# RMSNorm with SiLU on one core: stores moved to GpSimd's software queue, gamma's row in a tile of its own, three squares moved to VectorE

## The chip, the cores and the metric

One core of a Trainium2 chip. The metric is device time in microseconds (us) of one execution, lower is better. The span of a profile is the part between the first and the last instruction; it is 1.7 to 2.1 us shorter than the time of the same execution.

## The reference

```python
def setup_inputs():
    batch, seq_len, hidden = 8, 1024, 2048
    ...                      # x, gamma: normal float32; eps = 1e-5

def reference(x, gamma, eps):
    rms = np.sqrt(np.mean(x ** 2, axis=-1, keepdims=True) + eps)
    out = gamma * x / rms
    return (out * (1 / (1 + np.exp(-out)))).astype(np.float32)
```

So 67.1 MB are read, 67.1 MB are written, and each element needs a square, a scaling and a Silu.

## The kernel before

The 8192 rows are cut into 16 blocks of 512 rows (J = 4 rows on each of 128 partitions, 4.194 MB). A block is loaded by SyncE's queue into one of six buffers, worked on in place, and stored from the same buffer. A load of block b + 6 therefore waits for the store of block b.

```python
def sums(b, after_first=()):
    ss = small.tile([P, J], f32, name="ss")
    na = J // 2
    for j in range(na, J):                       # two rows on VectorE
        nc.vector.tensor_tensor_reduce(out=junk_v, in0=row(b, j), in1=row(b, j), ...,
                                       accum_out=ss[:, j:j + 1])
    for j in range(na):                          # two rows on ScalarE
        nc.scalar.activation(out=junk_a, in_=row(b, j), func=ACT.Square, accum_out=ss[:, j:j + 1])
        if j == 0:
            for s in after_first:
                store(s)                         # stands behind this square in ScalarE's queue
    ...                                          # rms = sqrt(ss / d + eps)

def finish(b, halves=False):
    for j in range(J):
        nc.vector.scalar_tensor_tensor(out=row(b, j), in0=row(b, j), scalar=rstds[b][:, j:j + 1],
                                       in1=g, op0=ALU.mult, op1=ALU.mult)
        if j % 2:
            cols = slice((j - 1) * d, (j + 1) * d)
            nc.scalar.activation(out=blocks[b][:, cols], in_=blocks[b][:, cols], func=ACT.Silu)
            if halves:
                nc.scalar.dma_start(out=ob[b][:, cols], in_=blocks[b][:, cols])

def store(b):
    nc.scalar.dma_start(out=ob[b], in_=blocks[b])
    if b + LEAD < nblk:                          # LEAD = 6
        load(b + LEAD)

...                                              # loads, gamma spread by a matmul, blocks 0 and 1
for b in range(1, last - 1):
    sums(b + 1, after_first=[b - 1])
    finish(b)
    invert(b + 1)                                # rstd = 1 / rms on VectorE
store(last - 2); finish(last - 1); store(last - 1)
sums(last); invert(last); finish(last, halves=True)
```

Before the change the row of gamma uses a sixth buffer of the block pool first, so the sixth load waits for it.

## Time and profile before

| | before |
|---|---|
| time, median of 3 runs | 317.48 us (317.22 to 317.64) |
| span of the profiled run (another execution, 318.03 us) | 316.3 us |
| VectorE (DVE) / ScalarE (ACT) busy | 223.5 / 223.8 us, 71% each |
| bytes moved by DMA | 134.25 MB, mean 425 GB/s |
| store to store in the middle | 19.35 us |

How to read it: an engine that is busy 71% can be idle because it waits for data or because it waits for another engine. The row of the DMA engines decides between these. It gives the mean busy share of 16 DMA engines per slice; a 9 says 90% or more, and the windows view gives the exact share. The lines are in the prediction.

### The profile page before, as it was taken

The numbers are of one execution on the slowest core, as the hardware profiler recorded it, in microseconds if no ns is written. First come the engines' busy times: TensorE is split into PE (matmuls) and PEld (weight loads), VectorE is DVE, ScalarE is ACT, GpSimd is POOL, SyncE is SP. The second block draws the span as 40 slices with busy tenths as digits, with TensorE's granted clock in tenths as the row PEclk, the third lists the DMA queues.
The fourth block names the chain that finished last, engine by engine and source line by source line (L and its number), as shares of the span: only waits on it lengthen the run. The fifth ranks groups of instructions, "written<-read, shape, count | busy, mean of one in ns | idle before, by whom it ended". The sixth has DMA issues, their size and how long they took to land.

```text
span 316.3 us, 444 instructions
## 1 busy us (share of the span) xinstructions
PE 2.1 (1%) x8; PEld 0.5 (0%) x8; DVE 223.5 (71%) x147; ACT 223.8 (71%) x144; POOL 0.2 (0%) x4
## 2 busy tenths in 40 slices
PE   0200000000000000000000000000000000000000
PEld 0000000000000000000000000000000000000000
DVE  0679499999493983939849397593966939993900
ACT  1357958999967777678676687676786776879540
POOL 0000000000000000000000000000000000000000
DMA  8999999999999999999999999999999999999996
GB/s 328 402 464 410 452 390 410 452 419 443 439 424 452 411 452 410 452 414 456 406 456 414 448 414 448 439 423 452 414 452 410 452 414 456 406 456 410 452 407 269
DMA packets 4763, 134.25 MB, mean 425 GB/s; under 512 B 532, under 2 KB 532, under 8 KB 536
## 3 DMA queue, kind: packets, MB, share of 16 engines
q1 hardware_dynamic: 2304, 67.11, 49.7%
q10 hardware_dynamic: 2456, 67.12, 49.2%
q14 instruction: 3, 0.02, 0.0%
HBM read 67.12 MB, written 67.11 MB: 424 GB/s over the span
## 4 chain that ended last, share of the span: by engine, by line
DMA 74%; DVE 14%; ACT 5%; issue 2%; DVEq 1%; ACTq 0%; SPq 0%
DMA xt<-in_x_dram 44%; DMA out_dram<-xt 30%; DVE xt L84 11%; ACT xt L88 3%; DVE junk_v L64 3%; ACT junk_a L68 1%; DVEq L164 1%; ACT L74 0%; ACT rms L74 0%; DVE rstd L79 0%; ACTq L93 0%; DVE ss L64 0%; SPq L52 0%; DVEq L64 0%; ACTq L74 0%
## 5 line engine op out<-in xcount | busy, mean ns | idle before, releaser
L84 DVE SCALAR_TENSOR_TENSOR xt<-xt,rstd,g 128x2048 f32<-128x2048 f32 x64 | 146.2, 2347 | 0.1
L88 ACT ACTIVATE xt<-xt 128x4096 f32<-128x4096 f32 x32 | 115.4, 3615 | 36.8 <-DVE xt L84 36.7
L64 DVE CUSTOM_DVE_ANT_0 junk_v<-xt 128x2048 f32<-128x2048 f32 x32 | 73.5, 2298 | 56.1 <-DMA xt<-in_x_dram 55.5
L68 ACT ACTIVATE junk_a<-xt 128x2048 f32<-128x2048 f32 x32 | 60.1, 1879 | 29.2 <-DMA xt<-in_x_dram 28.3
L74 ACT ACT_TABLE_LOAD x15 | 19.2, 1283 | 9.9 <-DVE ss L64 9.9
L88 ACT ACT_TABLE_LOAD x15 | 19.2, 1283 | 3.1 <-DVE xt L84 2.9
L79 DVE RECIPROCAL rstd<-rms 128x4 f32<-128x4 f32 x16 | 2.8, 172 | 11.3 <-ACT rms L74 11.3
L114 DVE COPY g<-junk_v 128x2048 f32<-128x2048 f32 x1 | 2.3, 2292 | 9.2 <-PE junk_v L112 9.2
L68 ACT ACTIVATION_READ_ACCUMULATOR junk_a<-xt 128x1 f32 x32 | 6.0, 186 | 0.0
L74 ACT ACTIVATE rms<-ss,eps_t 128x4 f32<-128x4 f32 x16 | 4.8, 297 | 1.2 <-DVE ss L64 1.1
L64 DVE DVE_READ_ACCUMULATOR2_ANT ss<- 128x1 f32 x32 | 4.5, 141 | 0.0
L112 PE MATMUL junk_v<-xt,ones 1*128 1x512 f32 x8 | 2.1, 1133 | 8.1 <-DMA xt<-in_gamma_dram 8.1
L107 ACT ACT_TABLE_LOAD x1 | 1.3, 1283 | 0.7 <-PEq L150 0.7
L105 DVE MEMSET ones<- 128x128 f32 x1 | 0.2, 165 | 0.8 <-PEq L150 0.8
L112 PEld LDWEIGHTS junk_v<-xt,ones 1*128 1x128 f32 x8 | 0.5, 306 | 8.1 <-issue 8.1
L107 ACT ACTIVATE junk_a<-ones 128x1 f32<-128x1 f32 x1 | 0.2, 174 | 0.0
L150 POOL MEMSET const-uint8-127<- 128x1 uint8 x1 | 0.1, 102 | 0.0
L150 POOL MEMSET const-bfloat16-1.0<- 128x1 bf16 x1 | 0.1, 101 | 0.0
L150 POOL MEMSET const-float32-0.0<- 128x1 f32 x1 | 0.1, 98 | 0.2 <-issue 0.2
L150 POOL MEMSET const-float32-1.0<- 128x1 f32 x1 | 0.1, 98 | 0.0
L106 DVE MEMSET eps_t<- 128x1 f32 x1 | 0.1, 59 | 0.0
## 6 DMA issues: line engine op xcount, KB each, us to landing
xt<-in_x_dram SPq DMA_DIRECT2D x16, 4096.0 KB, 42.0
out_dram<-xt ACTq DMA_DIRECT2D x15, 4096.0 KB, 35.2
out_dram<-xt ACTq DMA_DIRECT2D x2, 2048.0 KB, 10.4
xt<-in_gamma_dram ACTq DMA_DIRECT2D x1, 8.0 KB
```

The lines of the kernel that those rows point to most:

```text
L64: nc.vector.tensor_tensor_reduce(out=junk_v, in0=row(b, j), in1=row(b, j), scale=1.0, scalar=0.0, op0=ALU.mult, op1=ALU.add, accum_out=ss[ ...
L68: nc.scalar.activation(out=junk_a, in_=row(b, j), func=ACT.Square, accum_out=ss[:, j:j + 1])
L74: nc.scalar.activation(out=rms, in_=ss, func=ACT.Sqrt, scale=1.0 / d, bias=eps_t)
L79: nc.vector.reciprocal(out=rstd, in_=rmss.pop(b))
L84: nc.vector.scalar_tensor_tensor(out=row(b, j), in0=row(b, j), scalar=rstds[b][:, j:j + 1], in1=g, op0=ALU.mult, op1=ALU.mult)
L88: nc.scalar.activation(out=blocks[b][:, cols], in_=blocks[b][:, cols], func=ACT.Silu)
L105: nc.vector.memset(ones, 1.0)
L107: nc.scalar.activation(out=junk_a[:, 0:1], in_=ones[:, 0:1], func=ACT.Square)
L112: nc.tensor.matmul(junk_v[:, c * w:(c + 1) * w], ones[k:k + 1, :], grow[k:k + 1, 0:w], start=True, stop=True)
L114: nc.vector.tensor_copy(out=g, in_=junk_v)
L150: nc = _bacc.Bacc("TRN2", target_bir_lowering=False, num_devices=1)
L164: with _tile.TileContext(nc) as tc:
```

## The change

Its intent: ScalarE should no longer issue DMAs, a store should not wait behind a square whose block has not been loaded, the sixth load should not wait for gamma, and ScalarE should be relieved of three squares.

```diff
+    Q = 4
+    w = d // Q
+    grow = singles.tile([P, w], f32)
...
-        na = J // 2
+        na = 1 if b % 5 == 2 else 2
...
-                    nc.scalar.dma_start(out=ob[b][:, cols], in_=blocks[b][:, cols])
+                    nc.gpsimd.dma_start(out=ob[b][:, cols], in_=blocks[b][:, cols])

     def store(b):
-        nc.scalar.dma_start(out=ob[b], in_=blocks[b])
+        nc.gpsimd.dma_start(out=ob[b], in_=blocks[b])
...
-        grow = pool.tile([P, J * d], f32, name="xt")
-        for b in range(BUFS - 1):
+        for b in range(BUFS):
             load(b)
...
-        load(BUFS - 1)
```

(The cut lines only remove `Q` and `w` from their old place and replace `grow[..., 0:w]` by `grow[..., :]`.)

## The prediction

> **What bounds the kernel now.** I read the page first: busy shares, the 40 slices and the DMA queues; then the windows view with its DMA share; then the chain of waits; then the timeline of the start, of one steady block and of the end. From the page:
>
> ```profile
> PE 2.1 (1%) x8; PEld 0.5 (0%) x8; DVE 223.5 (71%) x147; ACT 223.8 (71%) x144; POOL 0.2 (0%) x4
> ...
> DMA  8999999999999999999999999999999999999996
> ...
> q1 hardware_dynamic: 2304, 67.11, 49.7%
> q10 hardware_dynamic: 2456, 67.12, 49.2%
> ```
>
> The reader is to see that VectorE (DVE) and ScalarE (ACT) are idle 29% of the span, while the DMA row is full in 38 of 40 slices and the two queues (q1 and q10) together take 98.9% of what 16 engines have. The windows view says the same for stretches of steady state (us, then the busy times, the clock, the DMA share and GB/s):
>
> ```profile
> 142.80:181.50 38.70, 0.00 (x0) 0.00 (x0) 27.60 (x18) 28.18 (x19) 0.00 (x0) 1.00 1.00 434
> 290.00:295.00 5.00, 0.00 (x0) 0.00 (x0) 3.23 (x3) 2.96 (x4) 0.00 (x0) 1.00 1.00 433
> 305.00:308.00 3.00, 0.00 (x0) 0.00 (x0) 0.00 (x0) 0.00 (x0) 0.00 (x0) 1.00 1.01 431
> 313.00:314.00 1.00, 0.00 (x0) 0.00 (x0) 0.00 (x0) 0.00 (x0) 0.00 (x0) 1.00 0.24 98
> ```
>
> The DMA share is 1.00 in the middle and still 1.00 with every compute engine idle, at 305 to 308 us. The last data packets are done at about 313.3 us; the last 3.0 us of the 316.3 us span are the acknowledgement and the end of the program. A block of 4.194 MB in and 4.194 MB out takes 19.35 us (successive stores are issued at 123.44, 142.80, 162.17, 181.52), that is 8.389 MB / 19.35 us = 433.5 GB/s. All 134.25 MB at that rate are **309.7 us**. Of the other 6.6 us of the span, 1.2 us are before the first packet, 3.0 us after the last, and some 2.4 us are slightly slower stretches (426 GB/s in 270 to 290 us, 419 in 40 to 60). The chain of waits goes from store to load and back through the reused buffers:
>
> ```profile
> 139.42 42.02 DMA xt<-in_x_dram
> 181.44 0.02 issue
> 181.46 0.03 ACT junk_a L68
> 181.48 0.04 issue
> 181.52 35.20 DMA out_dram<-xt
> ```
>
> A load needs 42.0 us and a store 35.2 us though either would take 4.194 MB / 433.5 GB/s = 9.7 us alone: both queue in a saturated DMA. The chain also shows why the author moved the store: it is issued only once the square of a later block may run, which waits for a load.
>
> **What the Trainium skill says.** (1) "DMA: Bandwidth & Descriptors", section "Where 436 GB/s comes from", puts the ceiling of the 16 ports at 435.2 GB/s; the 433.5 here is within 0.4% of it, so the trace agrees that there is no rate left to win. (2) The same page, "Queues, rings and completion order", says that each DMA engine takes turns between the queues that have work, a whole packet at a time. With both directions on hardware queues the trace agrees with an even split: at 36.67 us, when the first store is issued, the loads have had about 35.4 us x 0.43 MB = 15.2 MB; the six first loads are 25.2 MB, the missing 10.0 MB at half rate (0.217 MB per us) take 46 us, which gives 82.8 us, and the square of block 5 that had waited for its load starts at 84.02. How a packet of the software queue compares in size no run here shows yet. (3) The same page, "Latency and other measured facts", gives about 0.6 us to the first byte for the hardware queue and about 1 us for the software one: 0.4 us more per store; the trace has no software store. (4) "SBUF — State Buffer", section "SBUF: two separate sides", warns that VectorE in a two-port mode keeps GpSimd from writing its descriptors. The squares here take 2298 ns and the scalings 2347 ns for 2048 float32, about one element per ns, so they do not look like a doubled mode, and I expect no such stall; no run here shows it.
>
> **The change part by part.**
> - *Stores leave ScalarE's queue.* ScalarE loses 17 issues of 0.34 us = 5.8 us of its sequencer, all but one beside the DMA. In the end piece one stood on the chain of waits: the issue at 285.68 held the square of block 15 from 285.66 to 286.06, **0.4 us**. GpSimd gains 17 issues; it was idle (0.2 us busy). Each store pays about 0.4 us more to its first byte, perhaps 1 us with the hop to GpSimd (estimate from the skill's 1 us).
> - *A store no longer waits for a later load.* In steady state the second Silu of a block ends at 117.61 + 3.60 = 121.2, the store went at 123.44. Now it can start its data some 1.2 to 2.2 us earlier. It joins a queue that holds 35.2 / 19.35 = 1.8 stores already, so nothing is moved faster. At the start the Silu of block 0 ends at 32.70 and its store went at 36.67; now it is about 33.7, 3 us earlier. As the loads then share sooner, they land up to 3 us later, and later stores could come sooner by as much: the DMA does the same bytes in another order.
> - *Three squares on VectorE in blocks 2, 7 and 12.* VectorE gains 3 x (2.30 + 0.14) = 7.3 us, to 231 us; ScalarE loses 3 x (1.88 + 0.19) = 6.2 us, to 218 us. In a steady block VectorE has 13.8 of 19.36 us busy; with one square more it is 16.2, still 3.1 us under. Hidden. In block 2, in the ramp where VectorE is full (19.93 of 20 us at 40 to 60), it puts stores 1 and 2 some 2.4 us later, about what the earlier store 0 had won; both queues stay fed by the loads in hand.
> - *Gamma's row in its own tile.* The sixth load no longer waits for the row's use (4.8 us and 2.2 us in the waits of SyncE's queue). It stands behind five loads of 9.7 us each, 48 us of work, so it starts no sooner. Gain 0.
> - *End.* What counts is whether the last half store still finds the DMA busy. Before:
>
> ```profile
> 300.25 0.34 ACTq L90 DMA_DIRECT2D out_dram<-xt  x1
> 301.13 3.62 ACT L88 ACTIVATE xt<-xt 128x4096 f32<-128x4096 f32 x1 [0.91 <-DVE xt L84]
> 304.77 0.34 ACTq L90 DMA_DIRECT2D out_dram<-xt  x1
> ```
>
> It was issued at 304.77 and landed 10.2 us later at the earliest; 2.10 MB alone need 4.8 us plus about 2.3 us of start and acknowledgement, so it had some **3 us of slack** behind earlier stores. Shifts: -0.4 us (ScalarE's issue gone), +0.4 to 1 us (software queue), 0 to +2.7 us if loads land later by what store 0 gains. The sum, 0 to +3.3 us, is about the slack, so the end moves by 0 to 0.5 us.
>
> Sum: nothing from the steady state, nothing from the start, between -0.2 and +0.5 us at the end. From 317.48 I take **317.6 us**.
>
> **The rivals.**
> - *Stores get the larger share of the DMA.* If the software queue's packets hold several rows, a store drains fast and the loads wait. For: point (2) above leaves the size open. Against: in the page both hardware queues have one row of 32 KB per packet (2304 packets for 16 loads are 144 each, 128 rows and 16 small ones), and software may do the same. Then the last load lands when 16 loads and about 13.5 stores are through: 29.5 x 9.68 + 1.5 = 287 us, the one before at 267.7. From that landing VectorE needs 4.9 us (two squares), 9.1 us (block 13) and 9.3 us (block 14), to 291 us; before, it took from 282.0 to 304.77, 22.8 us, from there to the last issue, so now 313.8. Adding 1 + 4.8 + 2.3 + 1.3 us gives a span of some 323 us, a time of **324**, +2%.
> - *Loads get the larger share.* They land early, stores pile up, the DMA stays full to the end. The bound is then 309.7 + 1.2 + 3.0 plus the 1.2 us between span and time = 315.1 us; **315 to 317**.
> - *The software queue is slower as such* (descriptors written into on-chip memory, some DMA engines burdened by fetching them, or held up by VectorE). As all 16 engines carry equal bytes, one engine 2% slower sets the whole: 2% of 310 us is 6 us, **323 to 324**. For: it is the one new mechanism. Against: each descriptor moves 32 KB, so its own cost is small beside 32 KB / 27.1 GB/s = 1.2 us.
> - *A real gain.* If the late store were what starved the loads, issuing it early would cut the chain. Against: the DMA share of 1.00. Even with every gap but start and end gone the time is 315.1, -0.8%.
>
> **Range and chances.** The lower edge is just above the floor of 315.1; the upper one takes in most of a shared-out-of-balance tail. 315.4 to 322.0. Faster by over 2% means under 311.1, below the floor: 0.02. Slower by over 2% means over 323.8, what the first and third rivals reach only in full: 0.12. The rest, 0.86.
>
> **What would show it.** Right: a DMA share of 1.00 and 432 to 435 GB/s in the middle, 19.35 us from store to store, GpSimd issuing at the second Silu's end, VectorE near 231 us busy and ScalarE near 218, waits for loads merely shifted. Wrong: a lower rate in the middle (third rival); stores that land in 15 us with loads over 55 us and an idle DMA before the last store (first rival); or a rate above 435 GB/s, which would overturn the bound itself.

## The result, and the profile after

The changed kernel took **318.02 us** (median of 6 runs, 317.60 to 318.52), the kernel before 317.70 us (6 runs in all, 317.22 to 317.90). The ratio is 1.0012, with a 95% interval of 0.9999 to 1.0025: the same. Here and below a ratio is the mean time of one kernel's fast runs over that of the other's of the same rounds, so it isn't quite the ratio of the medians that are quoted.

The page of the changed kernel, the lines that answer to those of the prediction:

```profile
PE 2.1 (1%) x8; PEld 0.5 (0%) x8; DVE 230.5 (73%) x153; ACT 217.4 (69%) x138; POOL 9.4 (3%) x21
...
DMA  8999999999999999999999999999999999999996
...
q1 hardware_dynamic: 2304, 67.11, 49.7%
q0 software_dynamic: 2448, 67.11, 49.2%
```

VectorE has gained 7.0 us, ScalarE has lost 6.4 us, GpSimd (POOL) has 17 issues. The DMA row is digit for digit that of before, and the software queue q0 has taken the place of q10, with the same share. Its 2448 packets for 17 stores are 144 each, as on the hardware queues.

Windows of the changed kernel (columns as in the prediction: busy time of PE, PEld, DVE, ACT and POOL, clock, DMA share, GB/s):

```profile
159.20:197.90 38.70, 0.00 (x0) 0.00 (x0) 27.59 (x18) 28.20 (x18) 1.04 (x3) 1.00 1.00 434
305.00:308.00 3.00, 0.00 (x0) 0.00 (x0) 0.00 (x0) 0.00 (x0) 0.00 (x0) 1.00 1.01 431
313.00:314.00 1.00, 0.00 (x0) 0.00 (x0) 0.00 (x0) 0.00 (x0) 0.00 (x0) 1.00 0.43 180
```

The middle moves 434 GB/s as before, and the data end in the same microsecond, between 313 and 314. The timeline of its end:

```profile
298.65 0.53 POOL L93 DMA_DIRECT2D out_dram<-xt  x1 [13.51 <-ACT xt L91]
299.27 3.62 ACT L91 ACTIVATE xt<-xt 128x4096 f32<-128x4096 f32 x1 [0.91 <-DVE xt L87]
303.18 0.53 POOL L93 DMA_DIRECT2D out_dram<-xt  x1 [3.99 <-ACT xt L91]
```

The last half store is issued at 303.18, 1.6 us earlier than before (304.77), and lands 11.5 us later, where it had been 10.6 (this store alone, by the source view of its line; the 10.2 of the prediction is the other half store's). So it lands at 314.7 instead of 315.4. The last Silu ends 1.9 us sooner (302.89 against 304.75) and the kernel doesn't end sooner: the store waits longer in the DMA, and from its landing to the end of the span pass 1.5 us, where it had been 0.9. This last difference goes with the queue: 0.8 to 0.9 us in the profiles with stores on the hardware queue whose last landing is known (the kernel before, its quarter version and the hardware copy), 1.4 to 1.6 us in seven with stores on the software queue, and 1.9 us in the eighth (run 3).

The chain of waits, which had led through loads and stores before, puts 89% of the span of the changed kernel down to "issue", that is to nothing it can name. With the stores on GpSimd it no longer connects a store with the load that waits for it. A chain that breaks like this is no finding about the kernel. The issues of the page still show the queueing, first before (size of one, median us from issue to landing):

```profile
xt<-in_x_dram SPq DMA_DIRECT2D x16, 4096.0 KB, 42.0
out_dram<-xt ACTq DMA_DIRECT2D x15, 4096.0 KB, 35.2
```

and after:

```profile
xt<-in_x_dram SPq DMA_DIRECT2D x16, 4096.0 KB, 39.4
out_dram<-xt POOLq DMA_DIRECT2D x15, 4096.0 KB, 37.1
```

Load and store together stand in the DMA for 77.2 us before and 76.5 us after, or four blocks at 19.35 us.

### The profile page after: what moved, and what is told of

Its sections match the earlier page's. It is cut to its first block, busy times and chain, and to the rows that moved or that the text cites. A ratio compares the mean times of both kernels' runs of the same rounds, so it can differ in the third digit from the quotient of the medians.

```text
span 316.2 us, 463 instructions
## 1 busy us (share of the span) xinstructions
PE 2.1 (1%) x8; PEld 0.5 (0%) x8; DVE 230.5 (73%) x153; ACT 217.4 (69%) x138; POOL 9.4 (3%) x21
## 3 DMA queue, kind: packets, MB, share of 16 engines
q0 software_dynamic: 2448, 67.11, 49.2%
## 4 chain that ended last, share of the span: by engine, by line
issue 89%; DMA 4%; POOL 3%; POOLq 0%
DMA xt<-in_x_dram 4%; POOL out_dram L96 2%; POOLq L163 0%; POOL out_dram L93 0%; POOLq L96 0%; POOLq L93 0%
## 5 line engine op out<-in xcount | busy, mean ns | idle before, releaser
L67 DVE CUSTOM_DVE_ANT_0 junk_v<-xt 128x2048 f32<-128x2048 f32 x35 | 80.4, 2298 | 47.5 <-DMA xt<-in_x_dram 46.8
L71 ACT ACTIVATE junk_a<-xt 128x2048 f32<-128x2048 f32 x29 | 54.4, 1876 | 23.9 <-DMA xt<-in_x_dram 23.5
L96 POOL DMA_DIRECT2D out_dram<-xt x15 | 8.1, 542 | 276.6 <-ACT xt L91 276.6
L112 PE MATMUL junk_v<-grow,ones 1*128 1x512 f32 x8 | 2.1, 1131 | 8.3 <-DMA grow<-in_gamma_dram 8.3
L93 POOL DMA_DIRECT2D out_dram<-xt x2 | 1.1, 533 | 17.5 <-ACT xt L91 17.5
```

Source lines behind the costliest of these rows:

```text
L93: nc.gpsimd.dma_start(out=ob[b][:, cols], in_=blocks[b][:, cols])
L96: nc.gpsimd.dma_start(out=ob[b], in_=blocks[b])
L112: nc.tensor.matmul(junk_v[:, c * w:(c + 1) * w], ones[k:k + 1, :], grow[k:k + 1, :], start=True, stop=True)
```

## The experiments

My theory: the DMA is full, its bytes set the time, and what the change does to engines and issue times cannot be seen. The rivals: two effects cancel (the software queue costs something and the early stores or the moved squares win it back); or arithmetic and waits bind together with the DMA.

**1. The queue alone** (before, with the two `dma_start` lines on GpSimd).

```diff
-        nc.scalar.dma_start(out=ob[b], in_=blocks[b])
+        nc.gpsimd.dma_start(out=ob[b], in_=blocks[b])
```

> Only the issuing queue is changed: stores through GpSimd, squares and gamma as before. Theory (the DMA's 134.25 MB set the time, the software queue moves them as fast): 317.7 within 0.6 us, DMA share 1.00 in the middle at 433 to 434 GB/s. Rival (two effects cancel: the software queue costs something and the early stores or the moved squares win it back): clear of before by over 1 us (0.3%), in the opposite direction to the run with the rest alone.

317.74 us (5 runs, before 317.81), ratio 1.0002 (0.9990 to 1.0015). **2. The rest alone** (the changed kernel, with the same lines back on ScalarE):

> The squares and gamma's tile as in the changed kernel, stores back on ScalarE's queue where they were. Theory: 317.7 within 0.6 us. Rival (effects cancel): off by over 1 us, with the sign opposite to the queue alone.

317.51 us, ratio 0.9989 (0.9976 to 1.0003). Neither is a microsecond off, so there are no two effects of that size that cancel; effects of half a microsecond would stay within these intervals. Gamma's tile was never run apart from the squares. The queue-only trace also answers a question of the prediction. Its timeline has store 0, store 1 and the square that waited for the load of block 5:

```profile
33.07 0.67 POOL L93 DMA_DIRECT2D out_dram<-xt  x1 [32.63 <-ACT xt L88]
56.16 0.53 POOL L93 DMA_DIRECT2D out_dram<-xt  x1 [22.42 <-ACT xt L88]
...
84.17 1.88 ACT L68 ACTIVATE junk_a<-xt 128x2048 f32<-128x2048 f32 x1 [0.39 <-DMA xt<-in_x_dram]
```

In the kernel before the same square stands in the timeline as

```profile
84.02 1.88 ACT L68 ACTIVATE junk_a<-xt 128x2048 f32<-128x2048 f32 x1 [0.29 <-DMA xt<-in_x_dram]
```

Store 0 goes out 3.6 us earlier than before (36.67), yet the load lands at the same time, to 0.15 us. Store 1 cannot follow sooner (56.16, before 55.81), as its own Silu ends only then. What store 0 took from the loads early, they get back while the store queue is empty: from 56 to 60 us that queue moves 0.00 MB and the loads 1.57 MB, where before the stores had 0.59 and the loads 1.05 MB (DMA view of these windows). From 33 to 84 us the sums are alike again, 11.83 MB for loads and 9.93 for stores, before 11.76 and 9.86. In the stretch from 60 to 100 us the DMA queues of this trace had 51.4% of the engines for stores and 48.9% for loads; before, 51.0% and 49.0%. The software queue gets the same turn as the hardware one.

**3. Stores that go out late** (the changed kernel; a small copy in front of each whole-block store waits for the block three further on; the line that makes its one-column tile `gate` is cut).

```diff
+        if b + 3 < nblk:
+            nc.gpsimd.tensor_copy(out=gate, in_=blocks[b + 3][:, 0:1])
         nc.gpsimd.dma_start(out=ob[b], in_=blocks[b])
```

> The changed kernel, but each store waits until the load of the block three further on has landed (a copy of one column by GpSimd in front of it), so in the middle stores go out some 15 to 19 us later than in the changed kernel. Theory: with about three blocks still queued in the DMA it stays full, 318.0 within 1 us, DMA share 1.00 in the middle, store to store 19.35 us. Rival (the time of a store's issue matters, early stores hide a cost of the software queue): over 2 us slower than the changed kernel.

318.42 us (4 runs), ratio to before 1.0023 (1.0009 to 1.0037); the changed kernel has 1.0012. In its trace the store of block 7 is issued at 174.56 instead of 159.17, 15.4 us late. The issues of its page:

```profile
xt<-in_x_dram SPq DMA_DIRECT2D x16, 4096.0 KB, 28.9
out_dram<-xt POOLq DMA_DIRECT2D x15, 4096.0 KB, 28.3
```

Now 57.2 us or three blocks stand in the DMA instead of four, and that is still enough to keep it full (436 GB/s from 140 to 200 us). Stores issued 15 us later move the time by 0.1% against the changed kernel. Against the kernel before it is 0.2%, some 0.7 us, and this interval leaves 1 out: small, but not nothing.

**4 to 6. A quarter of the stores**: the DMA is relieved, with wrong results. Each store sends one row of four (83.9 MB in all): the kernel before, the changed kernel, and the kernel before with the queue alone changed. The last two stores, of half a block each, send half a row (their lines are cut).

```diff
-        nc.scalar.dma_start(out=ob[b], in_=blocks[b])
+        nc.scalar.dma_start(out=ob[b][:, 0:d], in_=blocks[b][:, 0:d])
```

> The kernel before, storing only a quarter of each block (wrong result on purpose): 83.9 MB instead of 134.2 MB. Theory (bytes bind the kernel, compute has room): at 433.5 GB/s the bytes need 193.5 us, so the bound passes to VectorE: 13.72 us per block as in the ramp of the kernel before, the last store issued near 249 us, time about 255 us (250 to 260). Rival (the stores' wait on a later load, or compute, binds): above 300 us.

> The changed kernel with the same quarter stores. Theory: with the DMA out of the way the three extra VectorE squares are on the path: 3 x 2.44 = 7.3 us more than the kernel before with quarter stores, about 262 us; the software queue itself within 1 us. Rival (GpSimd's early stores help once the DMA is free): as fast as or faster than the kernel before with quarter stores.

> The kernel before with the queue alone changed and quarter stores. Theory: within 1 us of the kernel before with quarter stores (the store's latency is off the path but for the last one; 0.4 us of ScalarE's issue gained, 0.4 to 1 us of first byte lost). Rival (the software queue is costly in itself, hidden only by the full DMA): over 2 us slower.

The kernel before takes 254.43 us, the changed one 261.98, the queue alone 255.33 (4 runs each; ratios to the full kernel before 0.8010, 0.8248 and 0.8040, each within 0.0014). Taking away bytes alone, with all arithmetic left, took away 63 us. Then the bound passes to the arithmetic, as this window of the quarter kernel before shows:

```profile
100.00:200.00 100.00, 0.00 (x0) 0.00 (x0) 99.76 (x66) 99.36 (x66) 0.00 (x0) 1.00 0.91 376
```

VectorE is busy 99.76 and ScalarE 99.36 of 100 us, and the DMA is no longer full (0.91). Here the changed kernel's extra squares on VectorE are on the path, though ScalarE is relieved of them. It is 7.6 us slower, of which the queue alone makes 0.9 us and the rest 6.7 us; three squares are 3 x 2.44 = 7.3 us. So in its own terms the change carries a cost that the full DMA hides.

The 0.9 us of the queue come from the end. Windows around the last store of the quarter kernel before,

```profile
249.00:250.00 1.00, 0.00 (x0) 0.00 (x0) 0.00 (x0) 0.06 (x1) 0.00 (x0) 1.00 0.09 37
250.00:251.00 1.00, 0.00 (x0) 0.00 (x0) 0.00 (x0) 0.00 (x0) 0.00 (x0) 1.00 1.01 410
```

and of the one with the queue changed:

```profile
249.00:250.00 1.00, 0.00 (x0) 0.00 (x0) 0.00 (x0) 0.18 (x1) 0.53 (x1) 1.00 0.00 0
250.00:251.00 1.00, 0.00 (x0) 0.00 (x0) 0.00 (x0) 0.00 (x0) 0.00 (x0) 1.00 0.45 184
251.00:252.00 1.00, 0.00 (x0) 0.00 (x0) 0.00 (x0) 0.00 (x0) 0.00 (x0) 1.00 0.84 340
```

The last Silu ends at 249.07 and 249.18; on the hardware queue the data move through the whole microsecond after 250, on the software queue they begin within it. GpSimd starts to issue 0.3 us after the Silu and takes 0.53 us instead of 0.34; the store lands 2.9 us after its issue instead of 2.6, and the span ends 1.5 us after that instead of 0.9. With the 0.1 us of the later Silu these make up the 1.3 us between the two spans (252.6 and 253.9 us; the profiled execution with the queue changed was the slowest of its four). So the largest part, 0.6 us, comes after the landing.

**7 and 8. The last store sent later**, to measure its slack (the changed kernel, with idle squares on ScalarE in front of the very last Silu).

```diff
+                if halves and j == 3:
+                    for _ in range(2):               # 5 in the second run
+                        nc.scalar.activation(out=junk_a, in_=blocks[b][:, 2 * d:3 * d], func=ACT.Square)
                 nc.scalar.activation(out=blocks[b][:, cols], in_=blocks[b][:, cols], func=ACT.Silu)
```

> The changed kernel with two idle squares (1.88 us each) on ScalarE before the very last Silu, 0.9 us of which fall into a gap: the last half store goes out some 2.9 us later. Theory (it waits behind earlier stores, slack some 3.9 us: data end 313.4, less 4.84 us of its own data, less about 1.5 us to its first byte, less the issue at 303.2): no change, within 0.6 us of the changed kernel. Rival (the compute chain of the end sets the time): +2.9 us.

> The same with five squares: the last half store some 8.5 us later. Theory: slack of 3.9 us used up, the time rises by about 4.6 us (3.5 to 6) over the changed kernel. Rival (compute chain): +8.5 us.

With two squares the time is 317.57 us, ratio to before 1.0000 (0.9984 to 1.0017): some 2.8 us of arithmetic more at the very end cost nothing (from the start of the block's first Silu to the last issue: 11.24 us, in the changed kernel 8.44). With five, 320.87 us, ratio 1.0104 (1.0081 to 1.0128), which is 0.92% or 2.9 us above the changed kernel's 1.0012. That is less than the 3.5 to 6 us that I expected. Windows of the run with five squares:

```profile
308.00:310.00 2.00, 0.00 (x0) 0.00 (x0) 0.00 (x0) 2.00 (x1) 0.00 (x0) 1.00 0.18 74
310.00:311.00 1.00, 0.00 (x0) 0.00 (x0) 0.00 (x0) 0.25 (x1) 0.46 (x1) 1.00 0.00 0
311.00:312.00 1.00, 0.00 (x0) 0.00 (x0) 0.00 (x0) 0.00 (x0) 0.08 (x1) 1.00 0.62 262
```

Here the DMA stands still, for about 3 us, and the time grows by as much. How large the slack is depends on what one counts from. The squares delay this execution's own arithmetic by 8.5 us, which gives 8.5 - 3.0 = 5.5 us. But its arithmetic stood 1.2 us earlier than in the profile of the changed kernel (first half store at 297.48 against 298.65), so the last store, at 310.55, is only 7.4 us later than the 303.18 there: 7.4 - 3.0 = 4.4 us. The 3.9 us that I expected had 1.5 us from issue to first byte; here the data begin some 0.8 us after the issue (at 311.38, if the engines are then full to 312). The last store, alone in the DMA, here took 6.5 us from issue to landing.

**9 and 10. The copy alone**: no arithmetic at all (wrong), each block stored as soon as it is loaded, on the hardware and on the software queue.

```diff
-        ...                                  # everything behind the loads
+        for b in range(nblk):
+            store(b)
```

> No arithmetic at all (wrong result on purpose): the same 16 loads and, on ScalarE's hardware queue, 16 stores of the same buffers, each as soon as its load has landed. Theory (the DMA's bytes set the time): the floor of the prediction, 315.1 us, within 1.5 us, so less than 1.2% under the full kernel. Rival (the waits between loads, arithmetic and stores cost the full kernel several per cent): under 308 us.

> The same copy with the stores on GpSimd's software queue. Theory (the software queue moves bytes at the same rate and only its last store pays, 0.9 us in the runs with quarter stores): the hardware copy plus 0 to 1 us. Rival (the software queue has a lower rate or another share, hidden in the full kernel): over 2 us more.

316.86 us on the hardware queue (ratio to before 0.9972, 0.9958 to 0.9985) and 317.29 us on the software queue (0.9992, 0.9979 to 1.0005). From the page of the hardware copy:

```profile
DMA  8999999999999999999999999999999999999997
```

Moving the data and doing nothing takes 99.7% of the time of the kernel before. What the software queue adds to the copy is 0.4 us between the medians, with intervals that overlap; but each of its five runs took longer than each of the five on the hardware queue. Its span again ends 1.4 us after the last landing, on the hardware queue 0.8.

The experiments point to no version with these transfers that beats both kernels by more than 0.3%: the copy has nothing left to take away but bytes. Other sizes or orders of transfers were not tried, and which part of the path between memory and buffers sets the rate is not shown.

## Why the prediction was right

The prediction said 317.6 us, and 318.02 was measured; it expected the same time because the DMA is full, and both of these held. Point by point:

- **The bound.** Shown from both sides. With all arithmetic gone, 0.3% is gone (the copy). With bytes gone, 63 us are gone (the quarter stores).
- **The floor of 315.1 us** was 1.8 us too low: the bare copy needs 316.9 us. In span it is 315.1 against 309.7 + 1.2 + 3.0 = 313.9 us, as I had put the whole transfer at the 433.5 GB/s of the middle, while the hardware copy too had only 428 GB/s from 13 to 100 us and 430 from 200 to 300. The other 0.6 us are the step from span to time, 1.8 us for the copy (316.9 - 315.1) where I had taken 1.2: the median of three runs less the span of another execution, whose own time was 318.03 us.
- **Steady state: no gain.** The stores are issued at 178.54 and 197.90, 19.36 us apart; before, 19.35. Run 3 shows that their moment hardly matters.
- **Squares: hidden.** The page says 230.5 and 217.4 us, where 231 and 218 were predicted. They are 6.7 us on the path as soon as the DMA is not full (quarter stores).
- **"Loads land up to 3 us later"** was the step that failed, though the end didn't feel it. The prediction put 0 to +2.7 us for it into its sum for the end; measured were 0.2 us at most with the queue alone, and the other sign in the changed kernel. In the run with the queue alone none of the ten loads that were waited for moved by more than 0.2 us (block 5: 84.17 against 84.02; block 6: 103.55 against 103.39; the last one waited for: 258.76 against 258.88). In the changed kernel the last one is even 1.3 us earlier (257.55). The extra square of block 2 delays stores 1 and 2 (58.45 and 72.40 against 55.81 and 69.78), as predicted, and it did more than offset the early store 0: from 33 to 84 us the loads had 12.58 MB, before 11.76. The run with the squares alone, where store 0 is not early (36.62), has 12.42 MB there and that last load at 258.23, so it is the squares that bring the loads forward.
- **The end.** The slack of the last store before was put at 3 us: 10.2 us to its landing less 7.1 us for the store alone. The last store took 10.6 us (10.2 was the other half store), and a store alone measured 6.5 us, though on the software queue; so 4.1 us (estimate from these two numbers). The test with five squares gives 4.4 to 5.5 us for the changed kernel, less 1.6 us for its earlier issue some 2.8 to 3.9 us (estimate). The profiles do not tell 3 from 4 us. The conclusion stands: neither 1.6 us earlier nor 2.8 us more arithmetic is seen. But the sum of 0 to +3.3 us did not come about; the issue moved by -1.6 us, mostly because the loads came earlier (1.3 us for the last one waited for) and not later.
- **The software queue's price.** 0.4 to 1 us per store was expected; 0.9 us was measured for the last one with the DMA free (in the profiles 0.6 of 1.3 us fall after the landing and not before the first byte), and 0.0 us (1.0002; by the interval -0.3 to +0.5 us) with it full. The stall of point (4) did not show: in the quarter run with the queue alone changed, where VectorE is busy 99.76 of 100 us, all 17 issues took 0.53 to 0.67 us, as in the software copy, where VectorE does nothing.
- **The rivals.** A larger share for the stores or for the loads: refused, 51.4% and 48.9%. A slower queue as such: refused, 434 GB/s in the middle and 0.4 us in the copy. A real gain: refused, ratio 1.0012.

Whether the 0.12% of the changed kernel over the one before is anything stays open: its interval includes 1.

## What to carry to other kernels

Divide the bytes by the rate of the steady middle before anything else. Here that was already 98% of the span, the DMA share was 1.00 with the arithmetic idle, and moving issues, waits and work between engines could not be seen as long as several transfers stood in the DMA; a copy without arithmetic confirmed it in one run. To find out what such a change really does, take bytes away until the DMA is not full: here a change that measured "same" turned out to cost 7.6 us of the 254 us of the relieved kernel. And the store at the end had slack for as long as others stood before it in the DMA; it is measured by delaying it, and by reading from the trace how much later it really went out.

## What the Trainium skill lacked or had wrong

- "DMA: Bandwidth & Descriptors", section "Where 436 GB/s comes from", says that for transfers between HBM and SBUF the HBM side binds at about 358 GB/s, though the same paragraph calls a measured 425 GB/s near the fabric's rate. Here one core, in a program that uses no other, moved 434 GB/s over long stretches, loads and stores together, close to the fabric's ceiling of 435.2 in the same section; 358 did not bind.
- The same page, "Queues, rings and completion order", has the engines take turns by packets, but doesn't compare the packets of a software and a hardware queue. Here 4.19 MB stores counted 144 packets on either kind of queue, and they shared with the loads 51.4% to 48.9%.
- The same page, "Latency and other measured facts", gives first-byte latencies of about 1 and 0.6 us, and has nothing on a difference after the landing. Here the span ended 0.8 to 0.9 us after the landing of the last store on the hardware queue and 1.4 to 1.9 us on the software queue. This is the largest part of what the kernel with quarter stores pays for the software queue (0.9 us between the medians; 0.6 of 1.3 us between the profiled spans); 0.3 us pass between the end of the Silu and the start of GpSimd's issue.
- No page says that the chain of waits loses its thread when stores go out through GpSimd: it put 89% of the span down to "issue".
